# A hybrid encoder block on one core: the block sums' transfers begun from GpSimd, and the row-tile sums of three pairs made on VectorE inside the out projection's loop

## The chip, the cores and the metric

The kernel runs on 1 core of one Trainium2 chip. The metric is the device time of one execution in microseconds (us); lower is better.

## What is computed

One layer of a bidirectional encoder on a sequence of 1024 tokens with 1024 channels, all in float32, then a final norm:

```python
h = rms_norm(x, mix_norm_w)
proj = h @ w_in                      # columns of three mixers and of three gates
y_dn, y_att, y_x = delta_net(...), block_gqa(...), cross_attention(...)
merged = sum over n of sigmoid(gate_n) * (y_n @ w_branch[n])
x = x + merged @ w_out
hf = rms_norm(x, ffn_norm_w)
x = x + square(relu(hf @ w_up)) @ w_down
return rms_norm(x, final_norm_w)
```

The mixer B (`block_gqa`) attends over the whole sequence with 8 heads, the mixer C (`cross_attention`) with 4 heads over 256 memory tokens.

## The kernel before

Every large product runs on TensorE (PE) as three matmuls on a high and a low part of each operand (`hi*hi + hi*lo + lo*hi`); ScalarE (ACT) rounds to the high part, VectorE (DVE) subtracts to get the low part (the helper `split`, lines 139 and 140). One pass over the stages, in order: norm and projections, convolutions and the delta rule (to about 590 us of the profiled span), the attention loop (590 to 1030 us), the three branch products and their gated sum (to about 1187), the out projection (to 1274), the up projection (to about 1620) and the down projection.

The two feed-forward products use a seven-product scheme (P1 to P7) on 2 by 2 blocks, so sums of blocks of their operands are needed.

**The block sums of `w_down`.** `block_sums(k, c)` (lines 1024 to 1032) makes one of 64 units: two loads from `w_down` into a tile `wc` of 128 partitions by 4 by 128 floats, four subtractions on GpSimd (POOL, line 1031), and one store to a DRAM tensor `wt_d`, which the down projection reads some 800 us later. The pool `wcp` has two buffers of `wc`. Loads and stores go through `ld` (line 97), which begins every transfer on SyncE (SP).

**The attention loop** (lines 1034 to 1060) runs 64 steps `t`. PE's order in it is pinned to the written one. A step has the scores of query tile `t+2`, every second step the output product `q_out`, one piece of the cross attention (`next(cr, None)`), 12 matmuls of the gates (`fill`), the transposes of step `t`, and one call of `block_sums`. The cross attention of each of its 4 heads begins with four loads into the single buffer `mkv` (lines 963 to 966); PE's first scores of a head read it. SP carries out its transfers in the order of its queue, and waits at a transfer until the buffer it writes is free or the tile it stores is made. Outside of the pinned parts a scheduler sets each engine's order.

**The branch products** (from line 1086): POOL adds the second and third branch to `g_acc` (line 1116), in tiles of `g_l`, which has two buffers.

**The out projection** (lines 1143 to 1161): for each of 8 row tiles `m`, two chains of 24 matmuls, DVE's add to the residual `x2` (line 1155), a store to `x2_d`, the norm factor (ACT's sum of squares, DVE's `rsq_t`, POOL's `rs` at line 136) and DVE's scaling (line 1158). From `m = 4` on, the blocks B11 and B21 of row tile `m - 4` are transposed on PE and split (`turned`). After the loop the sums of the four pairs (`m`, `m + 4`) are made, four operations each (lines 1169 to 1172): pairs 0 and 1 on POOL, pairs 2 and 3 on DVE. Two lead units of the up projection then run with 20 of those `turned` calls between their matmuls, PE pinned again. The same stage has POOL's sums of `w_up` blocks (`w_s`, lines 1195 to 1198).

Of the kernel before, what the change touches and what calls it, by code (L numbers as in the profile page):

```python
# [9 lines left out]
F32 = mybir.dt.float32  # L10
F32R = mybir.dt.float32r
AF = mybir.ActivationFunctionType
ALU = mybir.AluOpType
# [6 lines left out]
P = 128  # L20
# [66 lines left out]
def hybrid_block(tc, x, mem, mix_norm_w, w_in, dn_conv_w, dn_a_log, dn_dt_bias, dn_norm_w, q_norm_w, k_norm_w,  # L87
                 mem_norm_w, w_mem_kv, w_branch, w_out, ffn_norm_w, w_up, w_down, final_norm_w, ca_d, cb_d, rope_d,
                 out, dbg=None):
    nc = tc.nc  # L90
    pe, act, dve, gp = TensorE(tc), nc.scalar, nc.vector, nc.gpsimd
    def ld(out, in_):
        if out.dtype == F32R:
            out = out.bitcast(F32)
        if in_.dtype == F32R:
            in_ = in_.bitcast(F32)
        return nc.sync.dma_start(out=out, in_=in_)  # L97
# [4 lines left out]
    def pool(st, name, bufs=1, space=None, side=None):  # L102
        kw = {}
        if space is not None:
            kw["space"] = space
        if side is not None:
            kw["side"] = side
        if space is not DRAM:
            kw["reuse_waits"] = "tile"
        return st.enter_context(tc.tile_pool(name=name, bufs=bufs, **kw))  # L110
# [27 lines left out]
    def split(hi, lo, src, eng=None):  # L138
        act.copy(out=hi, in_=src)  # L139
        (eng or dve).tensor_tensor(out=lo, in0=src, in1=hi.bitcast(F32), op=ALU.subtract)  # L140
# [22 lines left out]
    def gemm(ps, pairs):  # L163
        for _ in gemm_steps(ps, pairs):
            pass

    def ld_rows(t, ap, m, c=slice(None), store=False):
        for h, j in enumerate((m, 15 - m)):
            a, b = t[h * 64:(h + 1) * 64, c], ap[j * 64:(j + 1) * 64, c]
            ld(out=b if store else a, in_=a if store else b)  # L170
# [27 lines left out]
    wt_d = [dram.tile([P, 4, 512], F32, name=f"wt_d{k}") for k in range(16)]  # L198
# [5 lines left out]
    def ps_mm():  # L204
        return pmm.tile([P, 512], F32, name="ps_mm", tag="mm")
# [14 lines left out]
    def norm_rs(xt, name, junkp):  # L220
        jk = junkp.tile([P, D], F32, name="jk", tag="jk", bufs=1)
        ss = sml.tile([P, 1], F32, name="ss", tag="ss")
        rs = sml.tile([P, 1], F32, name="rs", tag="rs")
        act.activation(out=jk, in_=xt, func=AF.Square, accum_out=ss)
        rsq(rs, ss, 1.0 / D, EPS)
        return rs
# [391 lines left out]
    turns = []  # L618
# [405 lines left out]
    def block_sums(k, c):  # L1024
        cs = slice(c * P, (c + 1) * P)
        w = wcp.tile([P, 4, P], F32, name="wc", tag="wc")
        for j in range(2):
            src = w_down[(2 * k + j) * P:(2 * k + j + 1) * P].rearrange("p (h c) -> p h c", h=2)
            ld(out=w[:, 2 * j:2 * j + 2], in_=src[:, :, cs])
        for o, a, b in ((0, 1, 0), (1, 3, 1), (3, 3, 0), (2, 2, 3)):  # L1030
            gp.tensor_tensor(out=w[:, o], in0=w[:, a], in1=w[:, b], op=ALU.subtract)  # L1031
        ld(out=wt_d[k][:, :, cs], in_=w)

    cr = cross()
    fill(24 * GATES[0])
# [7 lines left out]
    for t in range(NT):  # L1043
        if t + 2 < NT:
            q_scores(t + 2)
        if t % 2 == 0 and t:
            q_out(t // 2 - 1)
        next(cr, None)
        fill(FILL[0])
        q_trans(t, 0)  # L1050
        block_sums(t // 4, t % 4)
        fill(FILL[1])
        q_trans(t, 1)
        fill(FILL[2])
# [6 lines left out]
    sc = pool(top, "sc", bufs=2, side="right")  # L1061
# [12 lines left out]
    def ps2():  # L1074
        return pq.tile([P, 512], F32, name="ps2", tag="ps2")
# [4 lines left out]
    def ut(name, dt=F32, shape=(P, D), two=False):  # L1080
        return (U2 if two else U1).tile(list(shape), dt, name=name, tag="u2" if two else "u1")
# [50 lines left out]
    def turned(name, src, m):  # L1132

        if name not in hs:
            hs[name] = [[ut("hs", F32R, (P, 2, 512), two=name in ("B11", "B21", "T3", "T2")) for i in range(2)] for _ in range(2)]
        ps = ps_mm()
        for j in range(4):
            pe.transpose(ps[:, j * P:(j + 1) * P], src[:, j * P:(j + 1) * P], ident)
        pv = ps.rearrange("p (k t) -> p k t", k=4)
        for q in range(2):  # L1140
            split(hs[name][0][q][:, :, m * P:(m + 1) * P], hs[name][1][q][:, :, m * P:(m + 1) * P], pv[:, 2 * q:2 * q + 2])

    xs = []
    for m in range(8):
        f2 = m // 4
        t = slice((m % 4) * P, (m % 4 + 1) * P)
        x2 = ut("x2")
        xs.append(x2)
        ld_rows(x2, x, m)
        for f in range(2):  # L1150
            c = slice(f * 512, (f + 1) * 512)
            ps = ps2()
            gemm(ps, [(mgh[f2][k // 2][:, k % 2, t], mgl[f2][k // 2][:, k % 2, t], woh[k][:, c], wol[k][:, c])
                      for k in range(8)])
            dve.scalar_tensor_tensor(out=x2[:, c], in0=ps, scalar=0.5, in1=x2[:, c], op0=ALU.mult, op1=ALU.add)
        ld(out=x2_d[m], in_=x2)
        rs = norm_rs(x2, f"f{m}", sc)
        dve.scalar_tensor_tensor(out=x2, in0=x2, scalar=rs, in1=fwb, op0=ALU.mult, op1=ALU.mult)
        if m >= 4:
            turned("B11", xs[m - 4][:, 0:512], m - 4)  # L1160
            turned("B21", xs[m - 4][:, 512:1024], m - 4)


    turns = []
    for m in range(4):
        e = gp if m < 2 else dve
        b11, b21, b12, b22 = xs[m][:, 0:512], xs[m][:, 512:1024], xs[m + 4][:, 0:512], xs[m + 4][:, 512:1024]
        t3 = sc.tile([P, 512], F32, name="t3", tag="g_t")
        e.tensor_tensor(out=t3, in0=b22, in1=b12, op=ALU.subtract)
        e.tensor_tensor(out=b12, in0=b12, in1=b11, op=ALU.subtract)  # L1170
        e.tensor_tensor(out=b11, in0=t3, in1=b11, op=ALU.add)
        e.tensor_tensor(out=b21, in0=b21, in1=b11, op=ALU.subtract)
        turns += [("T3", t3, m), ("T2", b11, m), ("T1", b12, m), ("B22", b22, m), ("T4", b21, m)]

    o, ss3, rs3 = [None] * 8, {}, {}

# [250 lines left out]
```

## Time and profile before

| | us |
|---|---|
| median of 3 runs | 1926.17 |
| lowest, highest | 1922.19, 1927.29 |
| the profiled execution | 1923.72 |
| span of its instructions | 1921.9 |

The profiled execution is 1.82 us longer than its span (what lies around the instructions) and 2.45 us below the median. The profile gives, for each engine, its instructions with start and length, what each waited for, and the granted clock of TensorE. A busy PE is not PE at its best pace: matmuls overlap, so the pace is read from their starts.

### The profile page before, as it was taken

What the parts mean: (1) busy time and instruction counts of PE and PEld (TensorE: products, weight loads), DVE (VectorE), ACT (ScalarE), POOL (GpSimd) and SP (SyncE); (2) the same over time, 40 slices, a digit from 0 to 9 for tenths busy, and PEclk for the clock granted to TensorE, in tenths of its full rate; (3) what the DMA queues carried; (4) which work ended last, traced back from release to release, by engine and by line L of the source; (5) the groups of instructions that cost most, each with busy time, mean ns of one, the idle gap of its engine ahead of it and who ended that gap; (6) DMA issues with size and microseconds to landing.
All of it is one profiled execution on the core that took longest, in us unless ns stands there. A gap on an engine that the chain in (4) does not pass through costs nothing.

```text
span 1921.9 us, 27229 instructions
## 1 busy us (share of the span) xinstructions
PE 1827.6 (95%) x9891; PEld 1546.2 (80%) x9891; DVE 1237.4 (64%) x1795; ACT 808.2 (42%) x1597; POOL 532.4 (28%) x598
## 2 busy tenths in 40 slices
PE   6999999999999959869999999989999999999998
PEld 5888788988988848758888887867888888788886
DVE  4677989993676636646663456367787776555562
ACT  5453434653545636546663113133222223543341
POOL 1003131231343434442000052123656561011300
PEclk8999999998999979979999999999999999999999
DMA  7235664566656565564215545412454449666662
GB/s 152 71 106 165 196 200 138 160 181 187 186 150 197 167 187 171 179 190 146 88 55 167 201 150 183 135 66 80 147 179 142 159 174 350 240 206 201 203 198 66
DMA packets 340313, 313.28 MB, mean 163 GB/s; under 512 B 51986, under 2 KB 271314, under 8 KB 339667
## 3 DMA queue, kind: packets, MB, share of 16 engines
q1 hardware_dynamic: 339858, 311.02, 51.8%
q8 instruction: 78, 1.28, 0.3%
q10 hardware_dynamic: 320, 0.52, 0.1%
q14 instruction: 57, 0.46, 0.1%
HBM read 208.15 MB, written 103.32 MB: 162 GB/s over the span
## 4 chain that ended last, share of the span: by engine, by line
PE 82%; DMA 8%; DVE 5%; POOL 2%; issue 2%; ACT 1%; SPq 1%; POOLq 0%; ACTq 0%; DVEq 0%
PE ps L81 34%; PE ps_mm L81 30%; PE ps_dn L81 4%; PE ps_t L84 3%; PE ps_sm L81 3%; PE ps_t L81 2%; PE ps_s L81 2%; DMA wc<-in_w_down_dram 2%; PE ps_sp L81 2%; DMA wt_d<-wc 2%; SPq L97 1%; POOL wc L1031 1%; DMA xs_d<-dd 1%; DMA X<-xs_d 1%; DVE c_acc L412 1%
## 5 line engine op out<-in xcount | busy, mean ns | idle before, releaser
L81 PE MATMUL ps<-hs,ws 128*128 128x512 f32 x1344 | 312.6, 392 | 0.3 <-ACT hs L139 0.2
L81 PEld LDWEIGHTS ps<-hs,ws 128*128 128x128 f32 x1344 | 251.7, 189 | 52.0 <-ACT hs L139 0.8
L81 PE MATMUL ps_mm<-hTh,w_hi 128*128 128x512 f32 x704 | 286.6, 407 | 5.4 <-ACT hTh L139 4.8
L81 PE MATMUL ps_mm<-hTl,w_hi 128*128 128x512 f32 x704 | 284.4, 404 | 0.0
L81 PE MATMUL ps_mm<-hTh,w_lo 128*128 128x512 f32 x704 | 278.2, 395 | 3.1 <-DVE w_lo L140 3.1
L140 DVE TENSOR_TENSOR ab_lo<-ab_raw,ab_hi 128x1024 fp32r<-128x1024 f32 x112 | 139.7, 1296 | 94.4 <-issue 65.5
L1031 POOL TENSOR_TENSOR wc<-wc 128x128 f32<-128x128 f32 x256 | 127.7, 508 | 182.6 <-DMA wc<-in_w_down_dram 172.6
L139 ACT CAST ab_hi<-ab_raw 128x1024 fp32r<-128x1024 f32 x112 | 111.7, 1050 | 142.7 <-PE ps_mm L81 89.0
L81 PEld LDWEIGHTS ps_mm<-hTh,w_hi 128*128 128x128 f32 x704 | 134.3, 191 | 30.1 <-ACT hTh L139 5.0
L81 PEld LDWEIGHTS ps_mm<-hTh,w_lo 128*128 128x128 f32 x704 | 133.9, 190 | 29.1 <-DVE w_lo L140 3.3
L81 PEld LDWEIGHTS ps_mm<-hTl,w_hi 128*128 128x128 f32 x704 | 134.3, 191 | 20.8
L81 PE MATMUL ps<-ab_hi 128*128 128x512 f32 x336 | 129.9, 389 | 1.6 <-ACT ab_hi L139 1.6
L81 PE MATMUL ps<-ab_lo,ab_hi 128*128 128x512 f32 x336 | 130.6, 389 | 0.1
L81 PE MATMUL ps<-ab_hi,ab_lo 128*128 128x512 f32 x336 | 130.6, 389 | 0.0
L140 DVE TENSOR_TENSOR ptl<-ps_t,pth 128x512 fp32r<-128x512 f32 x128 | 86.5, 687 | 60.2 <-ACT pth L139 59.9
L139 ACT CAST w_hi<-w_raw 128x1024 fp32r<-128x1024 f32 x64 | 67.3, 1052 | 117.3 <-PE ps_mm L81 107.1
L140 DVE TENSOR_TENSOR w_lo<-w_raw,w_hi 128x1024 fp32r<-128x1024 f32 x64 | 83.0, 1298 | 41.6 <-ACT w_hi L139 40.7
L1116 POOL TENSOR_TENSOR g_acc<-g_acc,g_l 128x512 f32<-128x512 f32 x28 | 41.4, 1482 | 246.0 <-ACT g_yh L139 211.9
L139 ACT CAST pth<-ps_t 128x512 fp32r<-128x512 f32 x128 | 74.2, 586 | 51.1 <-PE ps_t L84 50.9
L901 DVE TENSOR_REDUCE nmx<-ps_s 128x1 f32<-128x1024 f32 x64 | 78.2, 1222 | 17.9 <-PE ps_s L81 17.0
L902 ACT ACTIVATE pm<-ps_s,nmx 128x1024 f32<-128x1024 f32 x64 | 71.7, 1120 | 41.1 <-DVE nmx L901 41.1
L84 PEld LDWEIGHTS ps_t<-ca,pm 128*128 128x128 f32 x512 | 64.1, 142 | 18.6 <-DVE cpl L140 1.4
(325 smaller groups left out, 4080.9 us busy)
## 6 DMA issues: line engine op xcount, KB each, us to landing
w_raw<-in_w_in_dram SPq DMA_DIRECT2D x50, 512.0 KB
ab_raw<-ab_d SPq DMA_DIRECT2D x96, 256.0 KB
w_raw<-in_w_up_dram SPq DMA_DIRECT2D x34, 512.0 KB
wc<-in_w_down_dram SPq DMA_DIRECT2D x128, 128.0 KB
wt_d<-wc SPq DMA_DIRECT2D x64, 256.0 KB
ab_d<-f_a SPq DMA_DIRECT2D x32, 512.0 KB
ab_raw<-wt_d SPq DMA_DIRECT2D x64, 256.0 KB
g_d<-gt SPq DMA_DIRECT2D x48, 256.0 KB
```

The lines of the kernel that those rows point to most:

```text
L81: return self._put(self.tc.nc.tensor.matmul(*a, **k))
L84: return self._put(self.tc.nc.tensor.transpose(*a, **k))
L97: return nc.sync.dma_start(out=out, in_=in_)
L139: act.copy(out=hi, in_=src)
L140: (eng or dve).tensor_tensor(out=lo, in0=src, in1=hi.bitcast(F32), op=ALU.subtract)
L412: dve.scalar_tensor_tensor(out=acc[:, o], in0=xn[:, i], scalar=cw[:, ct, j:j + 1], in1=acc[:, o], op0=ALU.mult, op1=ALU.add)
L901: dve.tensor_reduce(out=nmx, in_=ps, axis=AX.X, op=ALU.max, negate=True)
L902: act.activation(out=p_out, in_=ps, func=AF.Exp, bias=nmx, accum_out=sm)
L1031: gp.tensor_tensor(out=w[:, o], in0=w[:, a], in1=w[:, b], op=ALU.subtract)
L1116: (dve if bi == 2 and mt > 5 else gp).tensor_tensor(out=acc[mt][:, c], in0=acc[mt][:, c], in1=t, op=ALU.add)
```

## The change

Two edits. In `block_sums` the two loads and the store are begun from POOL (`gp.dma_start`) in place of SP. And the sums of the row-tile pairs become a function `sums(m)`, all on DVE, called for pairs 0, 1 and 2 at the end of the loop's steps 5, 6 and 7, and for pair 3 after the loop. The scratch tile of pairs 2 and 3 is now a tile of its own, `t3x`.

```diff
@@ block_sums @@
-            ld(out=w[:, 2 * j:2 * j + 2], in_=src[:, :, cs])
+            gp.dma_start(out=w[:, 2 * j:2 * j + 2], in_=src[:, :, cs])
         for o, a, b in ((0, 1, 0), (1, 3, 1), (3, 3, 0), (2, 2, 3)):
             gp.tensor_tensor(out=w[:, o], in0=w[:, a], in1=w[:, b], op=ALU.subtract)
-        ld(out=wt_d[k][:, :, cs], in_=w)
+        gp.dma_start(out=wt_d[k][:, :, cs], in_=w)
@@ the out projection @@
+    turns = []
+    t3x = sc.tile([P, 2, 512], F32, name="t3x", tag="g_l")
+
+    def sums(m):
+        b11, b21, b12, b22 = xs[m][:, 0:512], xs[m][:, 512:1024], xs[m + 4][:, 0:512], xs[m + 4][:, 512:1024]
+        t3 = sc.tile([P, 512], F32, name="t3", tag="g_t", bufs=2) if m < 2 else t3x[:, m - 2]
+        dve.tensor_tensor(out=t3, in0=b22, in1=b12, op=ALU.subtract)
+        dve.tensor_tensor(out=b12, in0=b12, in1=b11, op=ALU.subtract)
+        dve.tensor_tensor(out=b11, in0=t3, in1=b11, op=ALU.add)
+        dve.tensor_tensor(out=b21, in0=b21, in1=b11, op=ALU.subtract)
+        turns.extend([("T3", t3, m), ("T2", b11, m), ("T1", b12, m), ("B22", b22, m), ("T4", b21, m)])
...
             turned("B21", xs[m - 4][:, 512:1024], m - 4)
-
-
-    turns = []
-    for m in range(4):
-        e = gp if m < 2 else dve
...
+        if m >= 5:
+            sums(m - 5)
+
+
+    sums(3)
```

The order of SP's queue before, around the second head's `mkv` loads (`wc` and `wt_d` are the block sums' loads and stores, `w_raw` and `g_d` a gate's weights and result, `y_d` an output, `qh` queries):

```order
L97 DMA qh<-qs_d 128x2x256
L97 DMA wc<-in_w_down_dram 128x2x128
L97 DMA wt_d_204<-wc 512x1x128
L97 DMA wc<-in_w_down_dram 128x2x128 x3
L97 DMA wt_d_205<-wc 512x1x128
L97 DMA g_d_0_93<-gt 128x512
L97 DMA wc<-in_w_down_dram 128x2x128
L97 DMA w_raw<-in_w_in_dram 128x8x128
L97 DMA mkv<-mk_d 128x256
L97 DMA mkv<-mv_d 128x256
```

The same place of SP's queue with the change:

```order
L97 DMA y_d_125<-yt 128x256
L97 DMA qh<-qs_d 128x2x256
L97 DMA g_d_0_93<-gt 128x512
L97 DMA w_raw<-in_w_in_dram 128x8x128
L97 DMA mkv<-mk_d 128x256
L97 DMA mkv<-mv_d 128x256
```

All `wc` and `wt_d` transfers have left it. On POOL, before, the 256 subtractions stand alone between the delta rule's last operations and the branch sums:

```order
L844 TENSOR_TENSOR oacc_4610<-oacc_4610,o 128x512
L854 TENSOR_TENSOR o_rs<-o_ss,mhalf 128x4
L1031 TENSOR_TENSOR wc<-wc 128x128 x256
L1116 TENSOR_TENSOR g_acc<-g_acc,g_l 128x512 x28
L136 TENSOR_TENSOR rs<-rsq_t,mhalf 128x1 x5
```

With the change POOL has, in the middle of the loop, mostly pairs of units in this form, and behind the last store the same 28 branch sums:

```order
L1029 DMA wc<-in_w_down_dram 128x2x128 x4
L1031 TENSOR_TENSOR wc<-wc 128x128 x8
L1032 DMA wt_d_203<-wc 512x1x128
L1032 DMA wt_d_204<-wc 512x1x128
L1029 DMA wc<-in_w_down_dram 128x2x128 x4
...
L1032 DMA wt_d_214<-wc 512x1x128
L1116 TENSOR_TENSOR g_acc<-g_acc,g_l 128x512 x28
L136 TENSOR_TENSOR rs<-rsq_t,mhalf 128x1 x8
```

The four loads of two units now stand behind the two stores of the units before, and every subtraction behind them. On DVE, before, the sums of pair 2 (L1169 to L1172) begin after the last row tile's two adds (L1155), among the splits of the `turned` blocks:

```order
L1155 SCALAR_TENSOR_TENSOR x_12526<-ps_12555,x_12526 128x512
L140 TENSOR_TENSOR hs<-ps_mm,hs 128x2x128
L135 TENSOR_SCALAR rsq_t<-ss 128x1
L140 TENSOR_TENSOR hs<-ps_mm,hs 128x2x128 x3
L1169 TENSOR_TENSOR t_12618<-x_12444 128x512
L140 TENSOR_TENSOR hs<-ps_mm,hs 128x2x128
L1170 TENSOR_TENSOR x_12444<-x_12444,x_12144 128x512
L1158 SCALAR_TENSOR_TENSOR x_12526<-x_12526,rs,fwb 128x1024
L140 TENSOR_TENSOR hs<-ps_mm,hs 128x2x128
L1171 TENSOR_TENSOR x_12144<-t_12618,x_12144 128x512
```

With the change (lines 1150 to 1153 are the sums, 1168 the add, 1171 the scaling) the sums of a pair stand two row tiles earlier, here those of pair 1 around the adds of row tile 6:

```order
L1171 SCALAR_TENSOR_TENSOR x_12363<-x_12363,rs,fwb 128x1024
L1150 TENSOR_TENSOR t_12532<-x_12363 128x512
L1151 TENSOR_TENSOR x_12363<-x_12363,x_12081 128x512
L1168 SCALAR_TENSOR_TENSOR x_12450<-ps_12453,x_12450 128x512
L1152 TENSOR_TENSOR x_12081<-t_12532,x_12081 128x512
L1153 TENSOR_TENSOR x_12081<-x_12081 128x512
L1168 SCALAR_TENSOR_TENSOR x_12450<-ps_12479,x_12450 128x512
```

Pairs 0, 1 and 2 are made inside the loop, pair 3 alone behind it.

## Rows read from the trace of the kernel before

**Rows 1.** The page: span, chain that ended last (by engine), DMA queues.
```profile
span 1921.9 us, 27229 instructions
PE 82%; DMA 8%; DVE 5%; POOL 2%; issue 2%; ACT 1%; SPq 1%; POOLq 0%; ACTq 0%; DVEq 0%
q1 hardware_dynamic: 339858, 311.02, 51.8%
q10 hardware_dynamic: 320, 0.52, 0.1%
```

**Rows 2.** Busy time by stage: length, each engine's busy us, granted clock, DMA share.
```profile
590.00:1030.00 440.00, 398.66 (x2298) 341.35 (x2297) 265.27 (x418) 256.21 (x460) 127.72 (x256) 0.95 0.49 151
1240.00:1330.00 90.00, 77.30 (x369) 60.56 (x368) 54.66 (x102) 31.82 (x80) 29.24 (x23) 0.96 0.18 59
```

**Rows 3.** Waits in 570 to 1030 us: total us, times, longest.
```profile
POOL wc L1031 <- DMA wc<-in_w_down_dram: 172.6, 77, 15.8
PE ps_mm L81 <- DMA mkv<-mk_d: 41.2, 2, 21.7
```

**Rows 4.** PE's timeline at its two stops: start, us, idle before and its releaser.
```profile
692.26 0.28 PE L81 MATMUL ps_t<-ptl,vz 128*128 128x256 f32 x1
712.04 1.99 PE L81 MATMUL ps_mm<-mkv,cxq 128*128 128x256 f32 x6 [19.50 <-DMA mkv<-mk_d]
...
832.78 2.06 PE L81 MATMUL ps_mm<-mkv,cxq 128*128 128x256 f32 x6 [21.75 <-DMA mkv<-mk_d]
```

**Rows 5.** SP's timeline: issue start, us in all, transfers.
```profile
623.56 1.52 SPq L97 DMA_DIRECT2D wt_d<-wc  x2
626.11 1.25 SPq L97 DMA_DIRECT2D wc<-in_w_down_dram  x2
...
699.36 3.24 SPq L97 DMA_DIRECT2D wc<-in_w_down_dram  x3
703.65 0.56 SPq L97 DMA_DIRECT2D wt_d<-wc  x1
707.43 0.58 SPq L97 DMA_DIRECT2D mkv<-mk_d  x1
...
920.16 0.32 SPq L97 DMA_DIRECT2D mkv<-mk_d  x1
```

**Rows 6.** Busy time, the columns of rows 2, right after each stop.
```profile
712.04:718.05 6.01, 6.01 (x21) 4.83 (x22) 2.33 (x7) 2.66 (x6) 1.86 (x5) 0.53 0.51 155
832.78:836.90 4.12, 4.07 (x14) 3.38 (x15) 1.65 (x4) 1.15 (x1) 1.18 (x3) 0.50 0.70 217
```

**Rows 7.** The tile wc: instructions, duration min/median/max in ns, first and last start.
```profile
L1031 POOL TENSOR_TENSOR wc<-wc x256: 451/462/1457, 592.6 to 886.7; 128x128 f32<-128x128 f32 x128
L97 SPq DMA_DIRECT2D wc<-in_w_down_dram x128: 539/610/1482, 587.6 to 882.5; - x128
L97 SPq DMA_DIRECT2D wt_d<-wc x64: 555/567/573, 596.1 to 887.2; - x64
```

**Rows 8.** POOL's timeline: a unit's first subtraction, the last ones, the first branch sums.
```profile
628.66 0.47 POOL L1031 TENSOR_TENSOR wc<-wc 128x128 f32<-128x128 f32 x1 [4.17 <-DMA wc<-in_w_down_dram]
885.60 1.54 POOL L1031 TENSOR_TENSOR wc<-wc 128x128 f32<-128x128 f32 x3 [0.32 <-DMA wc<-in_w_down_dram]
1099.02 2.33 POOL L1116 TENSOR_TENSOR g_acc<-g_acc,g_l 128x512 f32<-128x512 f32 x1 [211.88 <-ACT g_yh L139]
1101.69 1.29 POOL L1116 TENSOR_TENSOR g_acc<-g_acc,g_l 128x512 f32<-128x512 f32 x1 [0.34 <-DVE g_l L1115]
```

**Rows 9.** Groups in 590 to 1030 us: busy us, mean ns.
```profile
L929 DVE TENSOR_SCALAR pm<-pm,rv 128x1024 f32<-128x1024 f32 x32 | 24.6, 768 | 1.1
```

**Rows 10.** Behind the out projection's loop: busy time, the columns of rows 2.
```profile
1273.80:1318.50 44.70, 32.00 (x162) 22.95 (x160) 32.21 (x63) 19.96 (x53) 13.06 (x9) 0.92 0.22 68
```

**Rows 11.** PE's timeline there: its two longest stops tied to DVE.
```profile
1283.83 0.63 PE L84 MATMUL ps_mm<-ca,x 128*128 128x128 f32 x4 [3.83 <-issue]
1286.82 1.09 PE L84 MATMUL ps_mm<-ca,x 128*128 128x128 f32 x4 [1.08 <-DVE hs L140]
```

**Rows 12.** DVE's timeline at the same place: the sums of pair 2.
```profile
1279.24 1.44 DVE L1170 TENSOR_TENSOR x<-x,x 128x512 f32<-128x512 f32 x1
1281.12 2.27 DVE L1158 SCALAR_TENSOR_TENSOR x<-x,rs,fwb 128x1024 f32<-128x1024 f32 x1 [0.44 <-POOL rs L136]
1285.33 0.68 DVE L1172 TENSOR_TENSOR x<-x 128x512 f32<-128x512 f32 x1
```

More of the change, by code (lines that the diff above doesn't have):

```diff
@@ L1161, in hybrid_block @@
             turned("B21", xs[m - 4][:, 512:1024], m - 4)
-    turns = []
-    for m in range(4):
-        e = gp if m < 2 else dve
[L1167 to L1173, printed above, removed]
+        if m >= 5:
+            sums(m - 5)
+    sums(3)
     o, ss3, rs3 = [None] * 8, {}, {}
```

## The prediction

> **What bounds the kernel now.** I read the chain that ended last first: 82% of the span lies on PE, 8% on DMA [rows 1]. So the kernel is bound by PE, and only what stops PE or slows its clock can move the time. The busy times by stage show where PE stops: in the attention loop it is busy 398.7 of 440 us, and around the end of the out projection 77.3 of 90 [rows 2]. These are the two places that the change touches.
>
> In the loop the table of waits puts nearly all of it to one cause: PE waited twice for the load of `mkv`, 41.2 us in total [rows 3]. PE's timeline shows them as idle times of 19.50 and 21.75 us [rows 4]. SP's timeline says why the load is late: the `mkv` load of the second head begins at 707.43, when PE had stood since about 692.5, and ahead of it in the queue stand loads and stores of the block sums, each of which waits for a buffer or for POOL (three loads take from 699.36 to 702.60) [rows 4, 5]. For the fourth head, when the block sums are over (the last at 887), SP begins the load at 920.16, and the waits name no third stop of that size [rows 3, 5, 8]. So SP's queue runs behind PE because of the block sums, and not for another reason.
>
> PE loses more than the idle time: after each stop the granted clock is about half (0.53 and 0.50, the lower of the two levels, 1.2 GHz in place of 2.4) for 6.01 and 4.12 us [rows 6].
>
> **What the change does, part by part.** *Block sums off SP.* SP loses 128 loads and 64 stores of 0.610 and 0.567 us [rows 7], 78.1 + 36.3 = 114 us of issue, and above all the waits between them. SP's issue time itself is not on the path. What remains ahead of `mkv` are gate results, outputs, queries and one weight load, as in the undisturbed case at 920. So both stops go: 19.50 + 21.75 = 41.25 us [rows 4]. The clock gives back 6.01 x 0.47 = 2.8 and 4.12 x 0.50 = 2.1 us [rows 6], 4.9 together. Part one: -46.1 us.
>
> *What POOL must now do.* POOL had spare time in the loop: 127.7 us busy of 440 [rows 2]. But it now runs the whole unit in one order: two stores, then four loads that wait for those stores to land, then eight subtractions that wait for the loads. The pace follows from that. A store takes 2.5 us from its issue to the next load that may use the buffer (623.56 to 626.11), of which 0.57 is issue, so 1.95 us to land; a load 2.55 us from its issue to the first subtraction (626.11 to 628.66), less 0.6 issue, again about 2 [rows 5, 7, 8]. The subtractions take 0.46 us each [rows 7]. With a price c for beginning one transfer on POOL, two units take c + 1.95 (first store lands) + 4c (loads) + 2.05 (last load lands) + 7 x 0.46 = 7.25 + 5c us; 32 such pairs from 588 on end at 820 + 160c.
>
> The trace of before does not show c: its transfers are all on hardware queues, SP's among them [rows 1], and POOL begins none. The low end is SP's row for the same transfers, 0.57; the high end the longest POOL instruction among these rows, 2.33 us [rows 8]. Ends that far apart I take in the middle by ratio, sqrt(0.57 x 2.33) = 1.15 us: the transfer is SP's, but the engine is one whose own instructions cost 0.46 us at least. Then POOL ends at 1004. The Trainium skill, DMA: Bandwidth & Descriptors, section Latency and other measured facts, gives about 1 us to the first byte for a transfer that GpSimd's software describes against 0.6 for SP's hardware; by that price POOL would end at about 980. No row here shows it.
>
> When is POOL needed next? Its queue has the branch sums behind the last store. The first ran at 1099.02 before, after an idle time of 211.88 us [rows 8]; with PE 46 us earlier it is due at 1053. The two buffers of `g_l` and the quick additions (1.29 against one every 2.7 us, start to start [rows 8]) let POOL be late by some 7 us (an estimate from those spacings), so the deadline is about 1060, which 820 + 160c meets for c up to 1.5. At 1.15 it does, by over 50 us: the cover is the idle time before 1099, and once it is gone each further 0.1 us on c costs 16 us of PE's time. Nothing else waits for these transfers before the down projection reads `wt_d`, except the first row-tile sum on DVE, whose scratch lies where `wc` lay; it stands behind the branch sums in time.
>
> *Row-tile sums.* Eight sums of about 1.3 us leave POOL, which is not on the path there. On DVE 12 sums of 0.68 us [rows 12] = 8.2 us are spread over the last three row tiles; with 54.7 of 90 us busy [rows 2], most of that behind the loop, I take them as hidden under the two chains of 24 matmuls of a row tile (uncovered they would cost at most 8.2). Behind the loop only pair 3 is left in place of pairs 2 and 3. There PE is busy 32.0 of 44.7 us, so idle 12.7, at clock 0.92, which loses another 32.0 x 0.08 = 2.6: at most 15.3 us can come back, at least 0 [rows 10]. I take what stands beside pair 2's sums: 3.83 and 1.08 us of idle time [rows 11], while DVE made those sums and a scaling that took 2.27 us [rows 12], plus 2.0 of the 2.6 us of clock: -6.9 us. The splits of the `turned` blocks stay and keep the rest.
>
> **The sum.** 46.1 + 6.9 = 53.0 us. The profiled execution of 1923.72 becomes 1870.7; the median of the three runs is 2.45 above that execution, so I expect 1873 us.
>
> **The rivals.** *POOL is too slow (slower).* The wait that leaves SP comes back as branch sums that start late: PE stops in the second branch once `g_l` and its accumulators are full. Lateness is 160 x (c - 1.5); it eats the whole gain of 53 at c = 1.83. At c = 2.0 POOL ends at 1140, 80 us late: 1873 + 80 = 1953 us. For it: POOL now does every step of a unit in one order, and its price per transfer is not in the trace. Against it: POOL's 211.88 us of idle time [rows 8], and that the price must be three times SP's. The Trainium skill, SBUF — State Buffer, section SBUF: two separate sides, says that GpSimd cannot write descriptions while VectorE holds the shared port in its two-port modes, and its next section, A bandwidth-pool intuition that's wrong, gives about 3.1 us for a transfer under such an instruction against 0.62 alone. Were every transfer like that, POOL would end at 1316 and the kernel take some 2130 us. The DVE instructions in the loop that could be of that kind, the 32 scalings of `pm`, last 24.6 us together [rows 9], and their whole length added to POOL would end it at 1029, still in time; so I leave the value at c = 1.15.
>
> *POOL is a little late.* With c from 1.5 to 1.83 part of the gain stays: 1873 to 1926, 1900 at c = 1.67.
>
> *`mkv` stays late.* If SP is held by something else, a gate's result or the single buffer, only the sums' part comes: 1926 - 7 = 1919. The 920.16 row speaks against it [rows 5]. That the change doesn't do what it says is excluded by the queues' order: SP has none of those transfers left.
>
> **How the numbers follow.** If c lies between 0.57 and 2.33 with even weight by ratio, it is below 1.5 in 69%, between 1.5 and 1.83 in 14%, above in 17%. Giving 6% to late `mkv` and a point more to the slow side for the port rule: forecast 0.64, a little late 0.12, late `mkv` 0.06, slower 0.18. A measurement of this kernel tells about 0.3% (6 us) from no change. Faster takes the forecast, most of "a little late" and most of late `mkv`: 0.77; no change gets 0.05, slower 0.18. The range leaves the slow case out: its top is late `mkv` and "a little late", 1922; its bottom is the whole 15.3 us of the second part in place of 6.9 (1865) less the 5 us by which runs of one kernel differ: 1860. The forecast alone would hold 1860 to 1882.
>
> **What would show it.** Right: no idle time of PE for `mkv` in the loop, granted clock 1.00 through it, SP's `mkv` loads begun before PE gets to their use; POOL's subtractions ending about 1000 and its first branch sum at about 1053, with no PE wait behind it; PE's stage behind the out projection some 38 us long. Wrong: POOL's last store later than 1060 with PE idle on `g_acc` or `g_l`; transfers on POOL that take over 1.5 us; the loop's stops still there; or the stage of 44.7 us unchanged, with its idle time on other splits.

## The result, and the profile after

The changed kernel takes 1872.0 us, the median of four runs (1870.27 to 1873.81), beside 1926.6 us of the kernel before on the same chip: a ratio of 0.9721, with a 95% interval of 0.9704 to 0.9739. The forecast was 1873 us. Run once more, on another occasion, it took 1871.45 us beside 1923.24, a ratio of 0.9728 (0.971 to 0.9746). The profiled execution took 1873.81 us.

First the page: the span, the DMA queues (packets, MB, share of 16 engines) and the chain that ended last by engine, which answer to [rows 1].

```profile
span 1872.0 us, 27157 instructions
q1 hardware_dynamic: 271250, 277.45, 47.4%
q0 software_dynamic: 11264, 33.57, 5.2%
PE 87%; DVE 5%; DMA 5%; issue 1%; ACT 1%; SPq 0%; POOL 0%; POOLq 0%; ACTq 0%; DVEq 0%
```

The block sums' 33.57 MB now go through a queue of their own, which POOL fills, and the share of DMA in the last chain has dropped from 8% to 5%. The busy time by stage, with the columns of [rows 2], for the attention loop and for the stage behind the out projection's loop (from 1 us before the up projection's first product, with the same 162 matmuls as in [rows 10]):

```profile
590.00:984.00 394.00, 393.96 (x2301) 338.37 (x2300) 267.24 (x420) 256.52 (x461) 260.80 (x441) 1.00 0.51 168
1225.50:1267.00 41.50, 32.68 (x162) 23.66 (x160) 29.26 (x59) 19.98 (x53) 12.52 (x9) 0.92 0.25 76
```

In the loop PE is busy all the time, at the full clock: the two stops of [rows 4] and the slow stretches of [rows 6] are gone. Nothing waits for the load of `mkv` any more. SP's timeline says why; here, as in [rows 5], a row is the start of an issue, its length and the transfer.

```profile
676.53 0.32 SPq L97 DMA_DIRECT2D g_d<-gt  x1
678.49 0.38 SPq L97 DMA_DIRECT2D w_raw<-in_w_in_dram  x1
679.40 0.32 SPq L97 DMA_DIRECT2D mkv<-mk_d  x1
```

The second head's load begins at 679.40, where it began at 707.43 before. Next POOL, with the columns of [rows 7]: what one of its transfers costs, and what its transfers waited for.

```profile
L1031 POOL TENSOR_TENSOR wc<-wc x256: 448/462/1486, 587.4 to 958.8; 128x128 f32<-128x128 f32 x128
L1029 POOL DMA_DIRECT2D wc<-in_w_down_dram x128: 702/720/1077, 582.3 to 954.6; - x128
L1032 POOL DMA_DIRECT2D wt_d<-wc x64: 694/737/1032, 590.6 to 959.6; - x64
  DMA wt_d<-wc: 61.0, 36
```

A load takes 0.720 us of POOL at the median and a store 0.737, none over 1.077. The 61.0 us are the waits of loads for the stores of the units before. POOL's timeline shows one pair of units from the middle, the last store, and the first branch sum (compare [rows 8]):

```profile
884.06 1.47 POOL L1032 DMA_DIRECT2D wt_d<-wc  x2
887.16 2.84 POOL L1029 DMA_DIRECT2D wc<-in_w_down_dram  x4 [1.62 <-DMA wt_d<-wc]
890.60 0.46 POOL L1031 TENSOR_TENSOR wc<-wc 128x128 f32<-128x128 f32 x1 [0.60 <-DMA wc<-in_w_down_dram]
...
959.57 0.75 POOL L1032 DMA_DIRECT2D wt_d<-wc  x1 [0.29 <-POOL wc L1031]
1050.10 2.36 POOL L1116 TENSOR_TENSOR g_acc<-g_acc,g_l 128x512 f32<-128x512 f32 x1 [89.77 <-ACT g_yh L139]
```

POOL ends its transfers at 960 and then stands idle for 89.77 us, waiting for the branch's operands: it is not what is waited for. Last, the two longest stops of PE behind the out projection (compare [rows 11]):

```profile
1233.66 1.09 PE L84 MATMUL ps_mm<-ca,x 128*128 128x128 f32 x4 [1.99 <-issue]
...
1254.17 1.08 PE L84 MATMUL ps_mm<-ca,x 128*128 128x128 f32 x4 [1.45 <-DVE hs L140]
```

The longest is 1.99 us where it was 3.83. The stage takes 41.5 us where it took 44.7, at the same granted clock of 0.92.

Two anchors place the gain. PE's first score of the attention loop starts 2.2 us earlier than before and its last 48.9 us earlier (958.2 against 1007.1), so the loop is 46.7 us shorter. (The first score starts anywhere from 583.7 to 592.9 in the traces of this case, so the 2.2 us are no gain of either edit.) The up projection's matmuls (`ps<-hs,ws`) reach from 1226.5 to 1555.1, 328.6 us, and reached from 1274.8 to 1606.7, 331.9 us: 3.3 us from the second edit in this pair of traces. The experiments show why this pair understates it.

### The profile page after: what moved, and what is told of

The parts are those of the page before. It is cut to its first block, busy times and chain, and to the rows that moved or that the text cites. A ratio compares the mean times of both kernels' runs of the same rounds, so it can differ in the third digit from the quotient of the medians.

```text
span 1872.0 us, 27157 instructions
## 1 busy us (share of the span) xinstructions
PE 1820.0 (97%) x9891; PEld 1541.2 (82%) x9891; DVE 1247.7 (67%) x1803; ACT 807.5 (43%) x1597; POOL 662.0 (35%) x782
## 3 DMA queue, kind: packets, MB, share of 16 engines
q0 software_dynamic: 11264, 33.57, 5.2%
## 4 chain that ended last, share of the span: by engine, by line
PE 87%; DVE 5%; DMA 5%; issue 1%; ACT 1%; SPq 0%; POOL 0%; POOLq 0%; ACTq 0%; DVEq 0%
PE ps_mm L81 34%; PE ps L81 33%; PE ps_t L84 4%; PE ps_dn L81 3%; PE ps_t L81 3%; PE ps_sm L81 3%; PE ps_s L81 3%; PE ps_sp L81 2%; DMA xt<-in_x_dram 1%; DMA X<-xs_d 1%; DMA xs_d<-dd 1%; DMA w_raw<-in_w_out_dram 1%; DMA w_raw<-in_w_mem_kv_dram 1%; DVE c_acc L412 1%; SPq L97 0%
## 5 line engine op out<-in xcount | busy, mean ns | idle before, releaser
L1029 POOL DMA_DIRECT2D wc<-in_w_down_dram x128 | 93.7, 738 | 74.1 <-DMA wt_d<-wc 61.0
L136 POOL TENSOR_TENSOR rs<-rsq_t,mhalf 128x1 f32<-128x1 f32 x26 | 15.7, 606 | 200.4 <-DVE rsq_t L135 193.1
```

Of the source, the lines that this page charges most:

```text
L136: gp.tensor_tensor(out=o, in0=tv, in1=mv, op=ALU.pow)
L1029: gp.dma_start(out=w[:, 2 * j:2 * j + 2], in_=src[:, :, cs])
```

## The experiments

All ratios are to the kernel before, run beside each kernel on the same chip. The first two make each edit alone.

**The transfers alone.**

```diff
-            ld(out=w[:, 2 * j:2 * j + 2], in_=src[:, :, cs])
+            gp.dma_start(out=w[:, 2 * j:2 * j + 2], in_=src[:, :, cs])
...
-        ld(out=wt_d[k][:, :, cs], in_=w)
+        gp.dma_start(out=wt_d[k][:, :, cs], in_=w)
```

> The kernel before with the block sums' transfers alone begun from POOL; the row-tile sums stay as they were. My theory (SP's order made mkv late, part one is worth 46 us): both stops of PE for mkv gone, 1926 - 46 = about 1880 us. Rival (the two edits need each other, or the stops' gain is given back later): less than 35 us, above 1891.

Measured: 1876.28 us (1874.76 to 1881.14) beside 1924.06, ratio 0.975 (0.9731 to 0.9769), that is -48 us. No wait of PE for `mkv` is left, and behind the out projection the wait that was 3.83 us before is still there (total us, times, longest):

```profile
PE ps_mm L84 <- issue: 5.7, 2, 3.7
```

So the first edit gives nearly all of the gain, and it does so in the loop.

**The sums alone.** The second edit of the change, with the transfers left on SP.

> The kernel before with the row-tile sums alone moved; all block-sum transfers stay on SP. My theory as predicted (6.9 us): about 1919 us. What the two traces suggest instead (the stage behind the out projection got 3.3 us shorter and 1.6 of that came back later): 1923 to 1924. Rival (the sums in the loop cost DVE something on the path): above 1926. The two mkv stops of about 41 us stay in every case.

Measured: 1916.55 us (1912.61 to 1924.46), ratio 0.9963 (0.995 to 0.9977): -7.1 us, between 4.4 and 9.6: the 6.9 us of the theory, and not the 1923 us that the first pair of traces suggested. The stops for `mkv` are still there, 40.2 us of them. The two edits add up within the intervals: 48 + 7.1 = 55 us, beside 53.8 and 52.3 by the two ratios of the change.

**Which of the sums.** Pair 2 alone is moved into the loop; pairs 0 and 1 stay on POOL.

```diff
+    two = sums(2, dve)
+    turns = sums(0, gp) + sums(1, gp) + two + sums(3, dve)
```

> The kernel before, with only the sums of row-tile pair 2 moved into the out projection's loop (on DVE, behind step 7); pairs 0 and 1 stay on POOL, pair 3 on DVE behind the loop, and the block-sum transfers stay on SP. If the gain of the second edit (7.1 us when made alone) is only pair 2's four sums leaving DVE's queue in the lead stage, as the prediction worked it out: 1917, -7 us. Rival: what counts is that pairs 0 and 1 leave POOL, which then has the norm factor of the last row tiles earlier: 1924, no gain. Between them, -3 us, both count.

Measured: 1918.81 us (1914.0 to 1923.48), ratio 0.9978 (0.9964 to 0.9991): -4.2 us, between 1.7 and 6.9. Pair 2 gives a gain of its own, which the rival denies. Whether pairs 0 and 1 add to it stays open: the intervals of the two runs overlap.

The traces say where this gain lies. The table compares all kernels that leave the rest of the up projection alone; the stage is the one behind the out projection's loop, as above, with 162 matmuls in each trace.

| traces | up projection's matmuls, us | the stage, us | granted clock in it |
|---|---|---|---|
| six without the sums: before, transfers alone, `mkv` from POOL and from ACT, and the two kept orders on SP (below) | 331.9 to 336.2 | 44.7 to 49.0 | 0.82 to 0.92 |
| pair 2 alone | 328.3 | 41.1 | 0.92 |
| four with all the sums: the change twice, the sums alone, the later POOL (below) | 327.0 to 328.6 | 39.8 to 41.5 | 0.92 to 0.96 |

In the mean the sums make the stage 6.3 us shorter (46.8 to 40.5), and the up projection's matmuls too (334.0 to 327.7). The trace of the kernel before has the shortest stage and the shortest up projection of the six, which is why the first pair of traces shows only 3.3 us.

**The `mkv` loads on POOL.** The block sums stay on SP; only the 16 loads of `mkv` move.

```diff
-                ld(out=mkv[:, i], in_=mk_d[i][:, h])
+                gp.dma_start(out=mkv[:, i].bitcast(F32), in_=mk_d[i][:, h])
```

> The kernel before with only the 16 loads of mkv moved from SP to POOL; all 192 block-sum transfers stay on SP. Theory A (mkv alone has no slack, only its place in SP's queue made PE stop): stops gone, about 1880 us, though SP runs as late as before. Rival B (everything on SP is late, and the next of SP's loads, queries or weights, stops PE instead): gain below 25 us, above 1901. Rival C (the DMA engines were full and no queue helps): no gain, about 1926.

Measured: 1930.2 us (1923.34 to 1936.04), ratio 1.0026 (1.0008 to 1.0045), no gain. The waits of PE and POOL's timeline:

```profile
PE ps_mm L81 <- DMA mkv<-mk_d: 44.6, 4, 24.4
```

```profile
710.09 1.52 POOL L1031 TENSOR_TENSOR wc<-wc 128x128 f32<-128x128 f32 x3 [0.35 <-DMA wc<-in_w_down_dram]
711.74 0.57 POOL L965 DMA_DIRECT2D mkv<-mk_d  x1
```

The load begins at 711.74, as late as on SP, because on POOL it stands behind the block sums' subtractions, which wait for SP's loads. So the time is near the 1926 us of Rival C, but the run separates none of the theories.

**The `mkv` loads on ACT.** The same edit, with `act.dma_start`.

> The kernel before, with only the 16 mkv loads begun from ScalarE's queue in place of SyncE's; all block-sum transfers stay on SP, in their old order. The former attempt to move mkv (to POOL) put it behind the block sums' subtractions and so settled nothing. Theory A (the load was late only because of what stood ahead of it in the same in-order queue): ACT's queue holds no block sum, so both stops of 19.5 and 21.8 us go or shrink under 3 us each, and with the clock 41 to 46 us come back: 1879 to 1886. Rival B (the load itself is late, through its single buffer, the DMA engines or PE's own progress, and only taking 33 MB of block-sum traffic out of SP's rings helped): the stops stay, 1920 to 1928. Rival C (ACT is in order too and stops at the load until the buffer is free, so its exponentials come late): the mkv waits go but PE waits on ACT in their place, 1900 or more.

Measured: 1933.2 us (1931.91 to 1933.88), ratio 1.0048 (1.003 to 1.0065). Rival C came, but not by the buffer. ACT's timeline, then PE's waits in the loop:

```profile
680.24 0.58 ACT L1016 COPY cyt<-ps_mm 128x512 f32<-128x512 f32 x1
701.46 0.33 ACTq L965 DMA_DIRECT2D mkv<-mk_d  x1
704.09 0.35 ACTq L966 DMA_DIRECT2D mkv<-mv_d  x1
704.48 0.58 ACT L139 CAST pth<-ps_t 128x512 fp32r<-128x512 f32 x1 [23.65 <-DMA wc<-in_w_down_dram]
```

```profile
PE ps_t L84 <- DVE ptl L140: 46.4, 3, 24.9
```

ACT stands from 680.8 to 701.46 at the first load of `mkv`, and the trace names a load of `wc` on SP as the releaser. The built program explains that. In it each transfer begun on SP or ACT counts its completion on one of eight counters (`DMAHW0` to `DMAHW7`), and the two engines share them; a transfer waits there for an earlier one that used its counter. These are two rows of ACT's order there and one of SP's, with their waits:

```
L965 DMA mkv_7507<-mk_d_101 128x256 [waits DMAHW7_49]
L966 DMA mkv_7507<-mv_d_102 128x256 [waits DMAHW1_49]
L97 DMA wc_8155<-in_w_down_dram 128x2x128 [waits DMAHW7_49]
```

The transfer that last used counter 7 before these is a block sums' store on SP, and on counter 1 it is a block sums' load; neither has a tile in common with `mkv`. So a load on ACT's queue was tied to the block sums all the same, and the stop moved from SP to ACT and from there, by the casts of `pth`, to PE. The Trainium skill, DMA: Bandwidth & Descriptors, section Anatomy of one DMA, says that a transfer's waits are made by the sequencer that issues it; ACT's 20.7 us agree.

**The order on SP.** Everything stays on SP, but the block sums' transfers and the `mkv` loads keep among themselves the order in which the program writes them.

```diff
+    def kept(out, in_):
+        return tc.keep_in_program_order(ld(out, in_))
...
-                ld(out=mkv[:, i], in_=mk_d[i][:, h])
+                kept(out=mkv[:, i], in_=mk_d[i][:, h])
...
-        ld(out=wt_d[k][:, :, cs], in_=w)
+        kept(out=wt_d[k][:, :, cs], in_=w)
```

> The kernel before, with the block sums' transfers and the mkv loads all on SP as before, but kept among themselves in the order in which the program writes them. In the kernel before, the scheduler put 25, 51 and 64 block-sum stores ahead of the second, third and fourth head's mkv loads; kept in order they are 16, 32 and 48, one per loop step. A unit takes about 4.7 us on SP (64 units from 587 to 887 us) and a step of PE's loop about 5.8, so that 25 units end at about 705, behind PE's need at 692, and 16 at about 665. Theory A (mkv is late because of how many block sums stand ahead of it, not because SP carries them): both stops go with SP carrying everything, 1876 to 1884. Rival B (SP cannot carry the block sums beside the rest, whatever the order; only another queue helps): stops stay or others come, 1915 or more. A+ : it also shows whether POOL is needed for it at all.

Measured: 1898.14 us (1896.65 to 1900.65), ratio 0.9877 (0.9857 to 0.9898), half of the way. PE's waits in the loop, SP's timeline and PE's timeline at the second head:

```profile
PE ps_mm L81 <- DMA mkv<-mk_d: 14.2, 6, 4.5
```

```profile
686.76 1.23 SPq L97 DMA_DIRECT2D wc<-in_w_down_dram  x2
690.02 0.33 SPq L97 DMA_DIRECT2D y_d<-yt  x1
690.39 0.43 SPq L97 DMA_DIRECT2D mkv<-mk_d  x1
```

```profile
693.07 0.50 PE L81 MATMUL ps_mm<-mkv,cxq 128*128 128x256 f32 x1 [4.51 <-DMA mkv<-mk_d]
```

The load is 17 us earlier than before but still about 2 us behind PE, now at all three heads, and behind an output `y_d` that is made only then. Neither theory had this: the order matters, but writing it down as it stands isn't enough.

**The order on SP, with `mkv` two steps earlier.** As the run before, but the next head's loads are written right behind the last product that reads the old `mkv`, and the output stores are kept in order too.

```diff
                 gemm(po, [(mvh[:, k], mvl[:, k], cph[:, k], cpl[:, k]) for k in range(2)])
+                if f and h < 3:
+                    nxt = load(h + 1)
```

> As e10 (all transfers on SP, in the written order, 1898 us), but the next head's mkv loads are written two loop steps earlier, right behind the last product that reads the old mkv, and the attention's output stores are kept in order with them; so 15 block-sum stores stand ahead of the second head's mkv and no output that is made later. In e10 the load began at 690.4, 2 us behind PE's need, and its three stops of 4.5 us with the clock behind them cost some 18 us. Theory A (only what stands ahead of mkv in the queue makes it late): the load begins at about 680, all stops go, 1876 to 1882, as much as the POOL transfers alone gave. Rival B (block sums on SP cost PE something else beside the place of mkv, so that only another queue gives it all): 1890 or more.

Measured: 1876.18 us (1874.64 to 1880.78) beside 1920.94, ratio 0.9772 (0.9749 to 0.9795). SP's timeline and the loop:

```profile
684.24 0.58 SPq L97 DMA_DIRECT2D mkv<-mk_d  x1
```

```profile
590.00:984.00 394.00, 393.63 (x2298) 337.42 (x2298) 266.33 (x419) 256.01 (x462) 133.56 (x256) 1.00 0.55 167
```

PE is busy for 393.63 of 394 us, with all block sums on SP and POOL at 133.56 us. Within the noise this is as good as the transfers from POOL alone (1876.28, ratio 0.975; the two intervals overlap). So what made `mkv` late was the work that the scheduler had put ahead of it in SP's order (25, 51 and 64 units' stores ahead of the second, third and fourth head's loads), not that SP carried it.

**A later POOL.** The changed kernel, with eight transfers a unit in place of three, each of 128 pieces.

```diff
-            gp.dma_start(out=w[:, 2 * j:2 * j + 2], in_=src[:, :, cs])
+            for i in range(2):
+                gp.dma_start(out=w[:, 2 * j + i], in_=src[:, i, cs])
...
-        gp.dma_start(out=wt_d[k][:, :, cs], in_=w)
+        for o in range(4):
+            gp.dma_start(out=wt_d[k][:, o, cs], in_=w[:, o])
```

> The changed kernel with each load of the block sums cut in two and each store in four: 8 transfers a unit on POOL in place of 3, the same bytes. It tests the rival 'POOL too slow'. If a transfer costs POOL 0.72 us whatever its size, 16 of them, 8 subtractions of 0.46 and some 3.5 us of landing make 18.7 us for two units, POOL ends at about 1180, some 120 us after the branch sums are due, and the kernel takes about 1990 us. If the price goes with the number of pieces (half or a quarter as many here), POOL ends at about 1070 and the kernel takes 1872 to 1890. If POOL's lateness does not reach PE at all: 1872 whatever POOL's end.

Measured: 1913.14 us (1910.52 to 1916.64), ratio 0.9934 (0.9911 to 0.9958), 41 us above the changed kernel. None of the three expectations came: a transfer of 128 pieces costs POOL 0.54 to 0.56 us, less than 0.72 but more than half of it, and POOL ends in between, at 1094. The tile `wc`, POOL's first branch sums, and PE's waits:

```profile
L1030 POOL DMA_DIRECT2D wc<-in_w_down_dram x256: 544/544/1027, 580.8 to 1085.6; - x128
L1034 POOL DMA_DIRECT2D wt_d<-wc x256: 537/561/946, 590.5 to 1093.6; - x128
```

```profile
1094.11 4.91 POOL L1118 TENSOR_TENSOR g_acc<-g_acc,g_l 128x512 f32<-128x512 f32 x4
```

```profile
PE ps_mm L81 <- DVE g_l L1117: 21.8, 1, 21.8
PE ps_mm L81 <- ACT g_yh L139: 10.4, 2, 8.7
```

The 41 us have two parts, and only one is POOL's. The first lies in the first branch, which has no sums on POOL. These are SP's first loads of that branch's operands and DVE's 16 results of it (first and last start), in the changed kernel and then here:

```profile
967.60 2.77 SPq L97 DMA_DIRECT2D y_raw<-y_d  x3
L1113 DVE SCALAR_TENSOR_TENSOR g_acc<-g_l,ps_mm x16: 679/687/689, 1005.7 to 1046.5; 128x512 f32<-128x512 f32 x16
```

```profile
1004.10 11.08 SPq L97 DMA_DIRECT2D y_raw<-y_d  x6
L1115 DVE SCALAR_TENSOR_TENSOR g_acc<-g_l,ps_mm x16: 681/686/689, 1022.3 to 1063.1; 128x512 f32<-128x512 f32 x16
```

In this kernel the scheduler put the loads of `y_raw` behind the last six gate results in SP's order, where in the changed kernel three of them stand ahead of those. PE waits 10.4 us for the rounded operands (`g_yh`), and the first branch ends 16.6 us later; the rest is smaller waits and the lower clock behind the stops (0.81 from 1010 to 1030). It is the effect of the `mkv` loads once more, at another place.

The second part is POOL's. With the first branch 16.6 us later its sums would be due at about 1067 (1050.10 + 16.6); they begin at 1094.11, 27 us late. PE stops once for 21.8 us, and behind the stop its clock is low:

```profile
1100.00:1110.00 10.00, 8.86 (x28) 7.11 (x29) 3.84 (x5) 1.92 (x2) 3.84 (x3) 0.68 0.54 188
1110.00:1140.00 30.00, 30.00 (x135) 24.82 (x134) 14.21 (x16) 3.54 (x5) 15.09 (x11) 1.00 0.42 136
```

The 28 matmuls behind the stop take 8.86 us, and at the pace of the second row they would take 6.2. That makes 21.8 + 2.6 = 24.4 us, and with the 16.6 it makes 41.0. So this is the slow rival, made real at a part of its size: POOL's queue has the deadline that the prediction gave it, and behind it nearly every microsecond of lateness reaches PE, 24 of 27 us here.

**Further on: the splits' buffers.** The changed kernel, with every second transposed block in the other PSUM pool; and the changed kernel again beside it.

```diff
-        ps = ps_mm()
+        flip[0] ^= 1
+        ps = ps2() if flip[0] else ps_mm()
```

> The changed kernel, with every second transposed block (28 turned calls in all) put into one of the six buffers of the other PSUM pool, so that PE need not wait for the split of the block before last. What is left of idle time in the lead stage is 8.8 us of 43, of which the waits for DVE's splits are 5.2 and the rest is for operations to issue, and the clock there is 0.92. If the two PSUM buffers set the pace: 3 to 8 us less than the changed kernel, 1864 to 1869. If DVE's work in the stage does (30 us busy of 43): within 2 us of it, 1870 to 1874. If the products lack their buffers: slower, 1875 or more.

> The changed kernel once more, on the chip of the three others, to have its ratio to the kernel before with a narrow interval: 1872, ratio 0.9721 within 0.002. The two edits made alone gave -47.8 and -7.1 us; if they add up with nothing shared, 1869; if the profiled pair of traces is right, which puts only 3.3 us to the second edit, 1873.

Measured: 1862.2 us (1860.97 to 1864.1), ratio 0.9681 (0.9663 to 0.9698), beside 1871.45 of the changed kernel. The stage from 1220 to 1265, first in the changed kernel, then here:

```profile
1220.00:1265.00 45.00, 36.42 (x177) 26.95 (x176) 32.53 (x64) 20.90 (x53) 12.52 (x9) 0.92 0.23 71
```

```profile
1220.00:1265.00 45.00, 39.92 (x215) 31.81 (x214) 38.34 (x77) 24.64 (x63) 12.40 (x9) 1.00 0.26 78
```

The same 45 us hold 215 matmuls in place of 177, at clock 1.00 in place of 0.92. So the two `ps_mm` buffers set the pace, and the gain is a little more than the 3 to 8 us expected; this version beats both kernels, by 9 us and by 61. The second run of the change lies between its two sums, 1869 and 1873, and tells neither from the other.

> The run e8 (every second transposed block into the other PSUM pool, 1862 us) with two of three blocks there. What is left of PE's stops between 1220 and 1265 is 5.1 us, of which 3.0 are for DVE's splits that hold a ps_mm buffer. If the two ps_mm buffers still set the pace: 1858 to 1860. If DVE's own work does (38.3 us busy of 45): 1861 to 1863. If the products now wait for buffers: 1864 or more.

Two of three blocks there gave 1864.16 us (1863.35 to 1865.74), ratio 0.97 (0.9682 to 0.9719), which can't be told from the run with every second one, since the intervals of the ratios overlap. No further gain shows, and what then sets the pace stays open.

> The run e8 (1862 us) with the block-sum transfers back on SP, kept in the written order with the mkv loads as in e10. If the order alone removes the stops: 1862 +- 3, and the transfers need not go to POOL. If SP's queue is too full even so: 1880 or more.

This one has the sums, the other PSUM pool and the plain written order on SP: 1887.77 us (1881.48 to 1890.8), ratio 0.9812 (0.979 to 0.9834). It keeps the three late loads, as the plain order did alone (PE waits 14.4 us for `mkv`). So the time is in the range of the second expectation, but not because SP's queue is too full: the run with the early loads shows that the same queue can carry them in time. The early loads weren't tried together with these edits.

## Why the prediction was right

**The first part, 46.1 us.** Both stops and the clock behind them came back: the loop is 46.7 us shorter in the trace, and the edit alone gave 48 with an interval of some 4 us to each side. Its reading of the cause, that SP's queue ran behind PE because of the block sums, is shown by the two runs with a kept order: with the same transfers on the same queue the stops shrink when fewer block sums stand ahead of `mkv`, and go when the load begins 7.7 us before PE's need (684.24 and 691.89). One thing it left out: the queue was not the only tie. The run on ACT shows that a load moved off SP can still wait for SP's transfers, by the shared counters. In the built program POOL's transfers have eight counters of their own, so the change met no such tie.

**POOL's price.** The guess of 1.15 us for a transfer was too high: 0.720 and 0.737, near SP's 0.610 and 0.567 [rows 7], so that the choice between the bounds should have leaned to the row of the same transfers and not to the longest sum. The formula 820 + 160c gives 937 for c = 0.73; POOL ended at 960. A store landed 2.9 us after its begin at the median (2.5 to 6.1), where 0.73 + 1.95 = 2.7 is what the formula has, and not all units went in pairs. The two errors cancel in part (960 beside 1004), and neither reached the time, because the cover held: 89.77 us of idle time were left. The first branch sum came at 1050.10, for which 1053 had been worked out.

**The slow rival** had the right place and the right deadline, as the run with eight transfers a unit shows; what failed it was its price, 2.0 us and more. The price of about 3.1 us, which it took from the Trainium skill, SBUF — State Buffer, section A bandwidth-pool intuition that's wrong, for a transfer under VectorE's two-port modes, did not come: of the 192 transfers 32 ran beside a scaling of `pm`, and they held POOL for 0.80 us in the mean and 1.077 at most, the others for 0.73. Whether those scalings are of that kind isn't shown. The price in the Trainium skill, DMA: Bandwidth & Descriptors, section Latency and other measured facts, 1 us to the first byte, would have ended POOL at 980 by that formula (an estimate), nearest of all to 960, though what it names is not the same span as POOL's 0.72 us of issue.

**The second part, 6.9 us.** Made alone it gave 7.1 (4.4 to 9.6), and the traces put 6.3 us of it into the stage that the prediction named. What was said to keep the rest, the splits of `turned`, did: PE's stops there are still put down to splits (5.2 us in nine) and to issue (3.1 in two), and another PSUM pool for half of the blocks gave 9 us. That the 12 sums cost nothing in the loop holds: from 1194 to 1225 PE is busy 31.00 of 31.00 us.

The two terms of the 6.9 us are less well borne out than their sum. Of the 4.9 us of idle time (3.83 and 1.08) that were to go, 3.9 went (12.7 to 8.8), and of the 2.0 us of clock nothing came back in that pair of traces. So the stage took 41.5 us there and not the 38 that was named as a sign. Over the six and four traces some 4 us are idle time and the rest is clock, which is lower without the sums (0.82 to 0.92) than with them (0.92 to 0.96). Why the clock there differs from trace to trace isn't shown. [rows 11] also needs care: the trace puts the 3.83 us to issue, which is no wait on DVE, and there are longer waits for splits in the stage than 1.08 (up to 1.45). That pair 2's sums cause the long stop is shown by the run that moves them alone, where the longest wait put down to issue is 2.0.

**The other rivals.** "`mkv` stays late" did not come; "a little late" needed c above 1.5.

## What to carry to other kernels

Where an engine waits for a small load, read what stands ahead of it in its queue, and how much earlier than its need the scheduler placed that: here moving the load's own place in the order gave as much, within the noise, as moving 192 other transfers away, and eight transfers a unit in place of three made another small load late in the same way. Another queue frees a transfer only if it has neither the old queue's work ahead of it nor its counters, so look at what the new queue is waiting for before the transfer moves. When work goes to an idle engine, find the next instruction that needs that engine; up to that time the price per piece hardly matters, and beyond it nearly every microsecond is PE's.

## What was not expected of the hardware

A transfer begun on POOL costs it 0.54 to 0.56 us when it has 128 pieces (eight a unit), and 0.72 to 0.74 us with 256 or 512 pieces: four times the pieces cost about a third more, so the price is mostly per transfer. The rate of the DMA engines was no part of the gain: the loop moved 168 GB/s with the block sums on POOL and 167 with all of them on SP. The Trainium skill, DMA: Bandwidth & Descriptors, section Rules for kernel authors, says that spreading transfers over the engines' queues gives no bandwidth and saves issue time only. The first half agrees with these two numbers. Issue time was not what was saved here: the run with everything kept on SP gained as much, by taking waits out of the load's way.
